# A hybrid decoder layer on one core: the convolution's norm written inside the value projection, and two weight blobs of the output projection read through the projections' staging buffers

## The chip, the cores and the metric

The kernel runs on one core of one Trainium2 chip. The metric is the device time of one execution in microseconds (us). An execution consists of the span that the profile shows, from the first to the last instruction, and about 2 us around it.

The engines that matter here are TensorE (PE in the profile, with PEld for its weight loads), VectorE (DVE), ScalarE (ACT) and SyncE (SP), which issues the weight loads. GpSimd (POOL) issues the transfers of the feed-forward part only. Each engine works through its own list of instructions in order and waits at an instruction whose operands aren't ready.

## The reference

One decoder layer, 512 tokens, width 2048, all in float32:

```python
h = modulate(rms_norm(x, norm1_g), sh1, sc1)
u = h @ w_in
u_b, u_c, u_h, q, kc, vc, ksl, vsl, kwn, vwn, gl = split(u)
y_conv = u_b * causal_depthwise_conv3(u_c * u_h)          # 1024 channels
y_attn = nsa_attention(q, k_cmp, v_cmp, k_slc, v_slc, k_win, v_win, sigmoid(gl))   # 8 heads x 128
mixed = concat([rms_norm(y_conv, gnorm_conv_g), rms_norm(y_attn, gnorm_attn_g)])
x = x + g1 * (mixed @ w_out)
h = modulate(rms_norm(x, norm2_g), sh2, sc2)
x = x + g2 * (square(relu(h @ w_ff1)) @ w_ff2)
return rms_norm(x, normf_g)
```

`sh1, sc1, g1, sh2, sc2, g2` are the six parts of `silu(c) @ w_ada + b_ada`.

## The kernel before

**Precision.** A float32 product is made of three fast matmuls. Each operand is split into a high part (`Copy` into the type fp32r on ScalarE) and a low part (the difference, on VectorE). `mm3` (L93 to L95) issues high x high, one mixed product and the other mixed product. A weight blob of 128 x 1024 (or 1072) numbers is therefore loaded by SyncE, copied by ScalarE (`wh`, L83) and subtracted by VectorE (`wl`, L84) before TensorE can use all of it.

**Staging.** In the first part of the kernel all weights go through one pool, `stage`: three `raw` buffers for the load (L73), two `wh` and two `wl`. A new load waits until a raw buffer has been read, and a new `wh` until TensorE is done with the blob two places before. In the last part (from L740 on) a second pool, `ffp`, has six `rw` buffers for the loads (L755) and three `hl` tiles for the split halves (`hilo`, L763 and L764). `ffp` is opened after the pools of the first part (`att`, `front`) are closed, and lies in the memory that they leave; a buffer of it that lies on an older one waits for the last use of that one.

**Who sets the order.** Up to L362 the program keeps the order in which it is written (`pin`). Behind that a list scheduler orders each engine's instructions; it takes the order of the source as a priority and moves single instructions past each other where it thinks them ready. Buffers are handed out from the free ones.

**The stages around the change.**

- The convolution (L487 to L514) makes eight channel tiles `y`, and adds their squares into `sacc`. The last projection of it ends the convolution's matmuls.
- `row_norm` (L167, called at L518 for the convolution) needs `sacc`: four small matmuls against a column of ones (L170), a square root on ScalarE with its table load (L177), a reciprocal (L178) and a diagonal tile `dg` (L188) on VectorE, one 512-column matmul that spreads the result over the partitions (L191), and a copy of it to `rc` (L181). `rc` is used by `mixed` (L555), eight VectorE instructions.
- The values and gates (L521 to L544): eight blobs of `w_v`, two groups `g` of four blocks `blk`, here called V0 to V7. A blob feeds 48 matmuls of 268 columns. With each blob the loop asks for one column of the modulation (`more_ada`: two loads of `w_ada` and two VectorE dot products, L133). Behind the fourth blob of a group the four banks are split into `vv` (L539, L540) and the gates are made (L543, with a table load for Tanh, and L544).
- The queries (L570 on), then the attention (L592 to L722), with 16 calls of `out_conv` (L602) spread over it; each call loads and splits one blob of `w_oc` and has 24 matmuls of 512 columns, and every second one also loads two tiles of `x` into a raw buffer, which L614 reads.
- Behind the attention its eight heads are normalized (L730) and split into `mixa` (L89, L90), with the last two calls of `out_conv`, 14 and 15, in between (L727 to L737).
- The attention's part of the output projection (L784 to L790): eight blobs of `w_oa`, here A0 to A7, each with 24 matmuls of 512 columns into eight banks. Then eight blobs of `w_oa2`, and the feed-forward part, which takes the larger half of the time.

The two loops that the change touches, before:

```python
    rc = accum("rc")
    row_norm(bank, sacc, 1024, rc)                                  # L518
...
    for k in range(8):
        wh, wl = hilo(hl_tile(), raw_blob(a["w_oa"][k]))            # L787
        for i in range(8):
            s = slice(i * P, (i + 1) * P)
            mm3(pm[i], wh[:, s], wl[:, s], mixa[k][:, 0], mixa[k][:, 1], k == 0, k == 7)
```

Of the kernel before, what the change touches and what calls it, by code (L numbers as in the profile page):

```python
# [40 lines left out]
def hybrid_layer(ctx: ExitStack, tc: tile.TileContext, a, out):  # L41
# [11 lines left out]
    def slot(dtype=F32, name="m"):  # L53
        return mainp.tile([P, SLOT], dtype, name=name, tag="m")

    def pair(dtype=F32, name="m"):
        return slot(dtype, name)[:, :2 * T].rearrange("p (a b) -> p a b", a=2)
# [4 lines left out]
    def accum(name="sacc"):  # L62
        return small.tile([P, T], F32, name=name, tag="acc2k", bufs=2)
# [3 lines left out]
    def pin(ins):  # L67

        return tc.keep_in_program_order(ins) if pinned[0] else ins

    def load(src, cols=1024):
        raw = stage.tile([P, BLOB], F32, name="raw", bufs=3)
        pin(nc.sync.dma_start(out=raw[:, :cols], in_=src))  # L73
        return raw

    def weights(src, cols=1024, spare=False):
        raw = load(src, cols)
        if spare:
            wh, wl = slot(F32R, name="swh"), slot(F32R, name="swl")
        else:  # L80
            wh = stage.tile([P, BLOB], F32R, name="wh")
            wl = stage.tile([P, BLOB], F32R, name="wl")
        pin(nc.scalar.activation(wh[:, :cols], raw[:, :cols], AF.Copy))  # L83
        pin(nc.vector.tensor_tensor(out=wl[:, :cols], in0=raw[:, :cols], in1=wh[:, :cols].bitcast(F32),  # L84
                                    op=OP.subtract))
        return wh, wl

    def split(dst, src):
        pin(nc.scalar.activation(dst[:, 0], src, AF.Copy))  # L89
        pin(nc.vector.tensor_tensor(out=dst[:, 1], in0=src, in1=dst[:, 0].bitcast(F32), op=OP.subtract))  # L90

    def mm3(ps, lh, ll, rh, rl, start, stop, more=False):
        pin(nc.tensor.matmul(ps, lh, rh, start=start, stop=False, skip_group_check=more))  # L93
        pin(nc.tensor.matmul(ps, lh, rl, start=False, stop=False, skip_group_check=more))  # L94
        pin(nc.tensor.matmul(ps, ll, rh, start=False, stop=stop, skip_group_check=more))  # L95
# [71 lines left out]
    def row_norm(bank, square, width, dst, t0=0, t1=NQ):  # L167
        total = bank()
        for t in range(t0, t1):
            nc.tensor.matmul(total[:, t:t + 1], square[:, t * P:(t + 1) * P], ones[:, 0:1],  # L170
                             start=True, stop=True)
        row_bcast(bank, total[:, t0:t1], width, dst[:, t0 * P:t1 * P])

    def row_bcast(bank, total, width, dst):
        n = total.shape[-1]
        rs = small.tile([P, NQ], F32, name="rs")[:, :n]
        pin(nc.scalar.activation(rs, total, AF.Sqrt, scale=1.0 / width, bias=eps))  # L177
        pin(nc.vector.reciprocal(rs, rs))  # L178
        ps = spread(bank, rs)
        if dst is not None:  # L180
            nc.scalar.activation(dst, ps[:, :n * P], AF.Copy)  # L181
        return ps
# [26 lines left out]
    def bank():  # L209
        return psp.tile([P, T], F32, name="ps")  # L210
# [104 lines left out]
    for s, (name, k) in enumerate(steps):  # L315
# [5 lines left out]
        wh, wl = w  # L321
# [41 lines left out]
    def more_ada(n, early=True):  # L363
        for _ in range(min(n, len(todo))):
            ada(todo.pop(0), early)
# [118 lines left out]
    sacc = None  # L484
    for j in range(8):
# [22 lines left out]
        if j == 0:  # L508
            sacc = accum()
# [5 lines left out]
    while background:  # L515
        tick()
    rc = accum("rc")
    row_norm(bank, sacc, 1024, rc)  # L518


    gates = attc.tile([P, NQ, NG, NR, 3], F32, name="gates")  # L521
# [1 line left out]
    for g in range(NG):  # L523
        pv = [bank() for _ in range(NQ)]
        for blk in range(4):
            wh, wl = weights(a["w_v"][g * 4 + blk], BLOB)
            more_ada(1)
            for j in range(4):
                k = blk * 4 + j
                s = slice(j * 268, (j + 1) * 268)  # L530
                for t in range(NQ):
                    c = slice(t * P, (t + 1) * P)
                    mm3(pv[t][:, :268], hs[k][:, 0, c], hs[k][:, 1, c], wh[:, s], wl[:, s],
                        k == 0, k == NK - 1)
        for t in range(NQ):
            if t % 2 == 0:
                vp = pair(F32R, name="vv").rearrange("p h (t c) -> p h t c", t=2)
            vv[g, t] = vp[:, :, t % 2]
            nc.scalar.activation(vv[g, t][:, 0], pv[t][:, :256], AF.Copy)  # L539
            nc.vector.tensor_tensor(out=vv[g, t][:, 1], in0=pv[t][:, :256],  # L540
                                    in1=vv[g, t][:, 0].bitcast(F32), op=OP.subtract)
            gt = gates[:, t, g].rearrange("p r b -> p (r b)")
            nc.scalar.activation(gt, pv[t][:, 256:268], AF.Tanh, scale=0.5)  # L543
            nc.vector.tensor_scalar(gt, gt, 1.0, 0.5, op0=OP.add, op1=OP.mult)  # L544
# [25 lines left out]
    for g in range(NG):  # L570
        pq = [bank() for _ in range(NR)]
        for k in range(NK):
            if k % 2 == 0:
                wh, wl = weights(a["w_q"][g * 8 + k // 2])
# [30 lines left out]
    def out_conv(m):  # L605
        if m % 2 == 0:
            x1.append(pair(name="x1"))
            out_conv.x = load(a["xt"][m // 2].rearrange("p a b -> p (a b)"))
        ps = psw.tile([P, T], F32, name="pw")
        wh, wl = weights(a["w_oc"][m])  # L610
        for k in range(8):
            s = slice(k * P, (k + 1) * P)
            mm3(ps, wh[:, s], wl[:, s], mix[k][:, 0], mix[k][:, 1], k == 0, k == 7)
        nc.vector.scalar_tensor_tensor(out=x1[m // 2][:, m % 2], in0=ps, scalar=col(M_G1, m),  # L614
                                       in1=out_conv.x[:, (m % 2) * T:(m % 2 + 1) * T],
                                       op0=OP.mult, op1=OP.add)
# [111 lines left out]
    for j in range(8):  # L728
        y = ya[j]
        nc.vector.scalar_tensor_tensor(out=y, in0=y, scalar=vec[:, V_GA + j:V_GA + j + 1], in1=ra,  # L730
                                       op0=OP.mult, op1=OP.mult)
        mt = pair(F32R, name="mixa")
        split(mt, y)
        mixa.append(mt)
        if j % 4 == 0:
            out_conv(m)
            m += 1  # L737
    att.close()
    front.close()

# [12 lines left out]
    def raw_blob(src):  # L753
        raw = ffp.tile([P, 1024], F32, name="rw", bufs=6)
        nc.sync.dma_start(out=raw, in_=src)  # L755
        return raw

    def hl_tile():
        t = ffp.tile([P, 2, 1024], F32R, name="hl", bufs=3)
        return t[:, 0], t[:, 1]  # L760

    def hilo(dst, src):
        nc.scalar.activation(dst[0], src, AF.Copy)  # L763
        nc.vector.tensor_tensor(out=dst[1], in0=src, in1=dst[0].bitcast(F32), op=OP.subtract)  # L764
        return dst
# [18 lines left out]
    sacc = accum()  # L784
    pm = [bankf() for _ in range(8)]
    for k in range(8):
        wh, wl = hilo(hl_tile(), raw_blob(a["w_oa"][k]))  # L787
        for i in range(8):
            s = slice(i * P, (i + 1) * P)
            mm3(pm[i], wh[:, s], wl[:, s], mixa[k][:, 0], mixa[k][:, 1], k == 0, k == 7)  # L790
# [212 lines left out]
    sacc = accum()  # L1003
# [193 lines left out]
```

## Time and profile before

| | |
|---|---|
| time, median of 3 runs | 2250.53 us (2250.18 to 2252.56) |
| the profiled execution's own time | 2251.69 us |
| its span | 2249.9 us |
| busy: VectorE, ScalarE | 1919.1 us (85%), 1009.5 us (45%) |
| moved by DMA | 453.62 MB, 202 GB/s in the mean |
| mean granted TensorE clock | 0.974 |

In a row of the timeline the first two numbers are the start and the duration in us, then come the engine, the line of the kernel, the operation, output and input tiles, shapes and the count of merged instructions; in brackets stand the engine's idle time before it and what ended that. Successive matmuls overlap: a row's duration is longer than the step from one matmul to the next. In a row of the table by stretches come the stretch, its length, the busy time (and count) of PE, PEld, DVE, ACT and POOL, the granted TensorE clock as a share of full speed, the DMA engines' share and GB/s.

### The profile page before, as it was taken

The page shows a single profiled execution, that of the slowest core. Times are in us where ns is not written, and L with a number is a line of the kernel's source. Part 1 is how long each engine was busy: PE and PEld are TensorE (multiplying, and loading weights), DVE is VectorE, ACT ScalarE, POOL GpSimd, SP SyncE. Part 2 cuts the span into 40 slices and gives each one's busy share as a digit, 9 for nine tenths or more (in the row PEclk, how much of TensorE's full clock was granted, in tenths as well). Part 3 has the DMA queues.
Part 4 walks back from the last instruction along what each step waited for, and adds up shares of the span by engine and source line. Part 5 has one row for each costly group of instructions (what it writes and reads, how often), then busy time and mean ns, then how long its engine had stood idle before and what let it go on. Part 6 is the DMA issues. An engine that isn't in the chain of part 4 may idle for free.

```text
span 2249.9 us, 37644 instructions
## 1 busy us (share of the span) xinstructions
PE 2138.4 (95%) x14942; PEld 1976.7 (88%) x14942; DVE 1919.1 (85%) x2998; ACT 1009.5 (45%) x1468; POOL 193.5 (9%) x366
## 2 busy tenths in 40 slices
PE   6999699999999999899999999999899999999996
PEld 4777478788877769799999999999899999999996
DVE  8889988776586755999999999999899999999995
ACT  4431233222354433766665666656433333333353
POOL 0000000000000000021111111113211011001100
PEclk8999799999999999899999999999999999999998
DMA  8988378756211134176666666668865466366432
GB/s 345 337 319 312 135 287 349 286 210 247 91 50 57 57 113 167 68 223 200 201 206 202 201 195 197 196 207 256 325 244 186 161 234 235 124 224 243 168 114 94
DMA packets 143984, 453.62 MB, mean 202 GB/s; under 512 B 15808, under 2 KB 20160, under 8 KB 143808
## 3 DMA queue, kind: packets, MB, share of 16 engines
q1 hardware_dynamic: 92192, 323.27, 40.2%
q0 software_dynamic: 51616, 127.95, 17.1%
q8 instruction: 117, 1.92, 0.3%
q14 instruction: 59, 0.48, 0.1%
HBM read 383.00 MB, written 68.16 MB: 201 GB/s over the span
## 4 chain that ended last, share of the span: by engine, by line
PE 78%; DVE 13%; ACT 4%; DMA 3%; issue 2%; SPq 0%; DVEq 0%; ACTq 0%
PE pf L93 19%; PE pf L95 19%; PE pf L94 19%; PE ps L95 5%; PE ps L94 5%; PE ps L93 5%; DVE scr L133 3%; DVE wl L84 2%; DMA wa<-in_w_ada 1%; PE pw L94 1%; PE pw L95 1%; PE pw L93 1%; DVE hl L764 1%; PE pt L683 1%; ACT wh L83 1%
## 5 line engine op out<-in xcount | busy, mean ns | idle before, releaser
L95 PE MATMUL pf<-tk,hl 128*128 128x256 f32 x3576 | 1007.1, 282 | 13.0 <-DVE hl L764 13.0
L93 PE MATMUL pf<-tk,hl 128*128 128x256 f32 x3576 | 1009.7, 283 | 9.6 <-ACT hl L763 8.2
L94 PE MATMUL pf<-tk,hl 128*128 128x256 f32 x3576 | 1007.1, 282 | 1.2 <-DVE tk L834 1.2
L95 PEld LDWEIGHTS pf<-tk,hl 128*128 128x128 f32 x3576 | 677.9, 190 | 15.6 <-DVE hl L764 15.5
L93 PEld LDWEIGHTS pf<-tk,hl 128*128 128x128 f32 x3576 | 679.2, 190 | 12.2 <-ACT hl L763 10.9
L94 PEld LDWEIGHTS pf<-tk,hl 128*128 128x128 f32 x3576 | 678.1, 190 | 1.6 <-DVE tk L834 1.5
L763 ACT ACTIVATE hl<-rw 128x1024 fp32r<-128x1024 f32 x266 | 280.8, 1057 | 291.6 <-PE pf L95 266.8
L764 DVE TENSOR_TENSOR hl<-rw,hl 128x1024 fp32r<-128x1024 f32 x266 | 324.5, 1221 | 48.4 <-ACT hl L763 48.0
L763 ACT ACTIVATE hl<-sg 128x1024 fp32r<-128x1024 f32 x189 | 200.4, 1061 | 268.6 <-PE pf L95 241.7
L764 DVE TENSOR_TENSOR hl<-sg,hl 128x1024 fp32r<-128x1024 f32 x189 | 230.8, 1222 | 42.2 <-ACT hl L763 42.1
L133 DVE SCALAR_TENSOR_TENSOR scr<-wa,cs 128x1024 bf16<-128x1024 f32 x192 | 229.7, 1220 | 6.2 <-DMA wa<-in_w_ada 6.1
L83 ACT ACTIVATE wh<-raw 128x1024 fp32r<-128x1024 f32 (+1 forms) x103 | 108.8, 1060 | 238.9 <-PE ps L94 137.9
L84 DVE TENSOR_TENSOR wl<-raw,wh 128x1024 fp32r<-128x1024 f32 (+1 forms) x103 | 126.2, 1227 | 54.9 <-ACT wh L83 54.1
L837 DVE TENSOR_TENSOR sg<-sg,rw 128x1024 f32<-128x1024 f32 x126 | 153.6, 1219 | 0.9
L95 PE MATMUL ps<-h_m,wl 128*128 128x512 f32 x360 | 143.0, 397 | 4.9 <-DVE wl L84 4.8
L93 PE MATMUL ps<-h_m,wh 128*128 128x512 f32 x360 | 142.6, 396 | 1.5 <-DVE part L346 1.0
L94 PE MATMUL ps<-h_m,wh 128*128 128x512 f32 x360 | 141.7, 394 | 0.0
L1011 DVE SCALAR_TENSOR_TENSOR x<-pf,mod,x 128x256 f32<-128x256 f32 x256 | 120.2, 480 | 15.6 <-PE pf L95 12.6
L95 PE MATMUL ps<-h,wl 128*128 128x512 f32 x280 | 114.4, 409 | 17.4 <-DVE wl L84 17.3
L93 PE MATMUL ps<-h,wh 128*128 128x512 f32 x280 | 113.3, 405 | 6.0 <-ACT wh L83 3.2
L94 PE MATMUL ps<-h,wh 128*128 128x512 f32 x280 | 113.1, 404 | 0.0
L977 POOL DMA_DIRECT2D g<-gt x192 | 100.9, 532 | 86.6 <-DVE gt L834 81.6
(306 smaller groups left out, 2971.9 us busy)
## 6 DMA issues: line engine op xcount, KB each, us to landing
rw<-in_w_f SPq DMA_DIRECT2D x262, 512.0 KB, 4.3
wa<-in_w_ada SPq DMA_DIRECT2D x192, 512.0 KB, 6.4
tk<-g POOLq DMA_DIRECT2D x114, 512.0 KB, 8.4
g<-gt POOLq DMA_DIRECT2D x192, 256.0 KB, 5.1
raw<-in_w_conv SPq DMA_DIRECT2D x32, 512.0 KB, 7.2
g<-gb POOLq DMA_DIRECT2D x36, 256.0 KB, 2.3
raw<-in_w_kv SPq DMA_DIRECT2D x16, 512.0 KB, 5.3
raw<-in_w_cv SPq DMA_DIRECT2D x16, 512.0 KB, 5.6
```

The lines of the kernel that those rows point to most:

```text
L83: pin(nc.scalar.activation(wh[:, :cols], raw[:, :cols], AF.Copy))
L84: pin(nc.vector.tensor_tensor(out=wl[:, :cols], in0=raw[:, :cols], in1=wh[:, :cols].bitcast(F32), op=OP.subtract))
L93: pin(nc.tensor.matmul(ps, lh, rh, start=start, stop=False, skip_group_check=more))
L94: pin(nc.tensor.matmul(ps, lh, rl, start=False, stop=False, skip_group_check=more))
L95: pin(nc.tensor.matmul(ps, ll, rh, start=False, stop=stop, skip_group_check=more))
L133: pin(nc.vector.scalar_tensor_tensor(out=scr, in0=w, scalar=1.0, in1=cs[i].rearrange("p a b -> p (a b)"), op0=OP.mult, op1=OP.mult, accum_ ...
L683: nc.tensor.transpose(pt[:, r * P:(r + 1) * P], probs[b, r][:, kb * P:(kb + 1) * P], ident)
L763: nc.scalar.activation(dst[0], src, AF.Copy)
L764: nc.vector.tensor_tensor(out=dst[1], in0=src, in1=dst[0].bitcast(F32), op=OP.subtract)
L837: nc.vector.tensor_tensor(out=dst, in0=x, in1=y, op=op)
L977: nc.gpsimd.dma_start(out=gd[p // 4][idx[j]][p % 4 // 2][:, p % 2], in_=g[:, j])
L1011: nc.vector.scalar_tensor_tensor(out=xm, in0=src, scalar=gate, in1=xm, op0=OP.mult, op1=OP.add)
```

## The change

The call of `row_norm` for the convolution moves from ahead of the value projection into its loop, behind the matmuls of V1. The first two blobs of `w_oa` are loaded and split with `weights`, that is through the buffers of `stage`, before the pools of the first part are closed; the loop over `w_oa` takes them from there and the other six as before. No arithmetic is added or left out.

```diff
@@ -515,7 +515,6 @@
     while background:
         tick()
     rc = accum("rc")
-    row_norm(bank, sacc, 1024, rc)
 
 
     gates = attc.tile([P, NQ, NG, NR, 3], F32, name="gates")
@@ -532,6 +531,8 @@
                     c = slice(t * P, (t + 1) * P)
                     mm3(pv[t][:, :268], hs[k][:, 0, c], hs[k][:, 1, c], wh[:, s], wl[:, s],
                         k == 0, k == NK - 1)
+            if g == 0 and blk == 1:
+                row_norm(bank, sacc, 1024, rc)
         for t in range(NQ):
             if t % 2 == 0:
                 vp = pair(F32R, name="vv").rearrange("p h (t c) -> p h t c", t=2)
@@ -735,6 +736,7 @@
         if j % 4 == 0:
             out_conv(m)
             m += 1
+    oa = [weights(a["w_oa"][k]) for k in range(2)]
     att.close()
     front.close()
 
@@ -784,7 +786,7 @@
     sacc = accum()
     pm = [bankf() for _ in range(8)]
     for k in range(8):
-        wh, wl = hilo(hl_tile(), raw_blob(a["w_oa"][k]))
+        wh, wl = oa[k] if k < 2 else hilo(hl_tile(), raw_blob(a["w_oa"][k]))
         for i in range(8):
             s = slice(i * P, (i + 1) * P)
             mm3(pm[i], wh[:, s], wl[:, s], mixa[k][:, 0], mixa[k][:, 1], k == 0, k == 7)
```

## The prediction

> **What bounds the kernel now.** I read the page, the chain that ended last, TensorE's timeline at both edited places, the stretches with their granted clock, and VectorE's, ScalarE's and SyncE's timelines there.
>
> ```profile
> span 2249.9 us, 37644 instructions
> PE 2138.4 (95%) x14942; PEld 1976.7 (88%) x14942; DVE 1919.1 (85%) x2998; ACT 1009.5 (45%) x1468; POOL 193.5 (9%) x366
> PE 78%; DVE 13%; ACT 4%; DMA 3%; issue 2%; SPq 0%; DVEq 0%; ACTq 0%
> ```
>
> TensorE is busy for 95% of the span and holds 78% of the chain. An edit pays where TensorE stands still or is slowed. The first place is the convolution's end:
>
> ```profile
> 461.00 0.39 PE L94 MATMUL ps<-h_m,wh 128*128 128x512 f32 x1
> 461.23 0.40 PE L95 MATMUL ps<-h_m,wl 128*128 128x512 f32 x1
> 464.49 1.26 PE L170 MATMUL ps<-ones,sacc 128*128 128x1 f32 x8 [2.87 <-DVE sacc L514]
> 467.04 2.07 PE L191 MATMUL ps<-dg,ones 128*128 128x512 f32 x2 [1.29 <-DVE dg L188]
> 468.12 1.21 PE L93 MATMUL ps<-wh,h 128*128 128x268 f32 x1
> 472.16 0.28 PE L93 MATMUL ps<-wh,h 128*128 128x268 f32 x1
> 499.86 0.29 PE L93 MATMUL ps<-wh,h 128*128 128x268 f32 x1
> 468.00:472.00 4.00, 4.00 (x16) 3.43 (x15) 4.00 (x10) 0.60 (x1) 0.00 (x0) 0.50 0.00 0
> 472.00:476.00 4.00, 4.00 (x35) 4.00 (x34) 3.26 (x7) 0.00 (x0) 0.00 (x0) 1.00 0.00 0
> ```
>
> The norm's matmuls stand ahead of V0 in TensorE's list, so V0 waits through their two waits (2.87 and 1.29 us). V0 then runs at half the granted clock until about 472: its first 15 matmuls take 472.16 - 468.12 = 4.04 us. The full-clock step is (499.86 - 472.16) / 225 = 0.123 us, 225 matmuls lying between V0's 16th and V5's first. 512-column matmuls step by 461.23 - 461.00 = 0.23.
>
> The second place is the start of A0:
>
> ```profile
> 817.20 0.40 PE L95 MATMUL pw<-mix,wl 128*128 128x512 f32 x1
> 822.66 0.80 PE L93 MATMUL pf<-mixa,hl 128*128 128x512 f32 x1 [5.07 <-ACT hl L763]
> 823.92 0.80 PE L95 MATMUL pf<-mixa,hl 128*128 128x512 f32 x1
> 830.48 0.40 PE L93 MATMUL pf<-mixa,hl 128*128 128x512 f32 x1
> 822.60:826.70 4.10, 4.00 (x9) 2.73 (x10) 3.50 (x3) 1.91 (x3) 0.00 (x0) 0.50 1.02 403
> ```
>
> TensorE idles 5.07 us for A0's high copy, again runs at half clock afterwards, and reaches A1 at 830.48.
>
> **The norm, part by part.** In the order of the built program V0 follows the convolution directly, the four L170 stand behind V1's 96th value matmul, and L191 behind 29 more. Nothing else is added; each engine's count is unchanged. Times below are on the old clock.
>
> ```profile
> 808.85 1.10 PE L191 MATMUL pt<-dg,ones 128*128 128x512 f32 x2
> 920.25 0.61 PE L170 MATMUL pf<-ones,sacc 128*128 128x1 f32 x4 [1.35 <-DVE sacc L773]
> 462.56 1.27 DVE L84 TENSOR_TENSOR wl<-raw,wh 128x1072 fp32r<-128x1072 f32 x1 [0.20 <-ACT wh L83]
> 466.90 1.22 DVE L133 SCALAR_TENSOR_TENSOR scr<-wa,cs 128x1024 bf16<-128x1024 f32 x1
> 468.04 1.22 DVE L133 SCALAR_TENSOR_TENSOR scr<-wa,cs 128x1024 bf16<-128x1024 f32 x1
> 476.47 1.10 ACT L83 ACTIVATE wh<-raw 128x1072 fp32r<-128x1072 f32 x1 [6.73 <-PE ps L95]
> 480.86 3.40 DVE L555 SCALAR_TENSOR_TENSOR y<-y,vec,rc 128x512 f32<-128x512 f32 x5
> 493.47 1.16 DVE L540 TENSOR_TENSOR vv<-ps,vv 128x256 fp32r<-128x256 f32 x3 [2.81 <-ACT vv L539]
> 494.19 1.28 ACT L543 ACT_TABLE_LOAD   x1
> ```
>
> Gain: V0 can start at 461.5, so its 16th matmul at 461.5 + 15 x 0.123 = 463.3 instead of 472.16: 8.8 us. About 2.2 of it (4.04 - 1.85) is the half clock.
>
> Paid back: at full clock four L170 records took 0.61, eight cost 1.0 to 1.2; L191 1.1. I take 2.1 together, which leaves 6.7.
>
> Do the splits keep up? V1's low half had been subtracted by 463.8 before; two dot products (468.04 - 466.90 = 1.14 each) and the last sum of squares, 0.6, now precede it: 466.7 at most, and V1 begins at 461.5 + 5.9 = 467.4. V3's copy and the square root's table load now stand ahead of the root on ScalarE: V1 ends at 473.3, copy 1.10, load 1.28, then the old 1.29 from sums to `dg`: 477.2. TensorE reaches L191 at 473.3 + 1.0 + 29 x 0.123 = 477.9. No wait, 0.7 us to spare.
>
> The new wait is at V5. V2 ends at 461.5 + 144 x 0.123 + 2.1 = 481.3. Behind that, in series: V4's copy to 482.6 and subtraction to 483.9; five `mixed` steps, now late because `rc` is, at 0.67 to 487.3; four `vv` subtractions to 488.8; a `mixed` step, 489.5; four gates, which wait for V3's end at 487.2, four copies and the Tanh load (1.28), to 489.9; two `mixed` steps, 491.2; two dots, 493.5; V5's subtraction, 494.7. TensorE gets to V5 at 493.1 and has four high matmuls there before it needs the low half, 493.6. The wait is 1.1 us; bounds 0 and 2.2 (the same chain with its idle moments squeezed out, or as many again). V6 to V7 have their halves over 2 us early. Part one: 6.7 - 1.1 = **5.6 us**, between 4.5 and 6.7.
>
> The Trainium skill ("TensorE: Matmul & The Clock Gate", "Part 1: The HAM clock gate", "What's actually happening") lets the clock fall to half after an idle window of about 3.4 us. Here gaps of 2.87 and 1.29 us with work between them were followed by 0.50, so the trace doesn't keep to it. By the rule alone the 2.2 us would have nothing to do with these gaps, part one would be 3.4 and the time 2241.2.
>
> **The two blobs.**
>
> ```profile
> 805.33 0.75 DVE L614 SCALAR_TENSOR_TENSOR x<-pw,mod,raw 128x512 f32<-128x512 f32 x1 [0.23 <-PE pw L95]
> 811.41 1.96 ACT L89 ACTIVATE mixa<-ya 128x512 fp32r<-128x512 f32 x3 [0.82 <-DVE ya L730]
> 813.88 1.28 DVE L90 TENSOR_TENSOR mixa<-ya,mixa 128x512 fp32r<-128x512 f32 x2
> 819.53 1.41 DVE L730 SCALAR_TENSOR_TENSOR ya<-ya,vec,rc 128x512 f32<-128x512 f32 x2
> 821.03 1.35 DVE L90 TENSOR_TENSOR mixa<-ya,mixa 128x512 fp32r<-128x512 f32 x2
> 821.57 2.94 ACT L763 ACTIVATE hl<-rw 128x1024 fp32r<-128x1024 f32 x3
> 822.64 3.50 DVE L764 TENSOR_TENSOR hl<-rw,hl 128x1024 fp32r<-128x1024 f32 x3 [0.25 <-ACT hl L763]
> L755 SPq DMA_DIRECT2D rw<-in_w_oa x1: 328/328/328, 817.6 to 817.6; - x1
> DMA to landing us min/median/max: 3.4/3.4/3.4
> ```
>
> A0's load waits for the raw buffer that L614 of `out_conv(13)` reads, so it starts at 806.1 and lands 3.4 later. Its high copy stands behind the first head's copy, 812.1 to 813.1, and moves the next two heads by about 1 us, which VectorE doesn't feel (it took them at 813.9 and later). A1's copy waits for `out_conv(15)`'s matmuls (817.6), and the copies of heads 6 and 7 queue behind it; they are wanted some 30 us later.
>
> The built order gives TensorE 14 high matmuls of A0 (seven banks, L93 and L94) right behind 817.20: 817.4 to 820.7. The first L95 needs A0's low half, which VectorE has placed behind the last two L730: 820.9 + 1.2 = 822.1. Ten matmuls remain: 822.1 + 2.3 = 824.4 for A1's start against 830.48. Gain 6.0 us. The idle shrinks to 1.4 us, and I take the clock to stay up; then some 2 us of the gain is the half-clock stretch.
>
> What is late next: A2's load. Its buffer lies on A0's staging memory and now waits for A0's last high matmuls, 824.4. It lands at 827.8; copy 1.0, subtraction 1.2: 830.1. A1 ends at 824.4 + 5.6 = 830.0 and A2's first L95 comes at 830.5. A3's load waits for A1's last matmul, leads a burst of five exactly like the row at 817.6, and gives its low half at 836.0; wanted at 836.1. I charge 0.1 for both. Upper bound from the next row below: a first landing of 4.8 instead of 3.4 makes each 1.4 later, 2.4 together after the spare time. From A4 on the waits for buffers are the old ones. Part two: **5.9 us**, between 3.6 and 6.0.
>
> **Sum.** 5.6 + 5.9 = 11.5. The rest is carried by a busy TensorE, with compute-released waits that shift along. The profiled execution took 2251.69 (span 2249.9 and 1.8 around it): 2240.2. The median of the runs is 1.16 lower, so I forecast **2239.0 us**.
>
> **The rivals.**
>
> ```profile
> 325.27 0.50 PE L95 MATMUL ps<-h,wl 128*128 128x512 f32 x1 [1.57 <-DVE wl L84]
> 327.00:329.00 2.00, 2.00 (x10) 1.65 (x9) 2.00 (x5) 1.71 (x2) 0.00 (x0) 1.00 0.40 160
> 703.28 0.38 PE L703 MATMUL pt<-ones,sr 128*128 128x1 f32 x2 [1.12 <-DVE sr L701]
> 704.00:711.00 7.00, 6.99 (x26) 5.85 (x26) 4.67 (x24) 2.55 (x10) 0.00 (x0) 0.51 0.00 0
> DMA to landing us min/median/max: 4.8/8.2/11.2
> ```
>
> A, the clock falls in the new waits. A lone gap of 1.57 us at 325 left the clock at 1.00, but 1.12 us at 703 among smaller ones brought 7 us at 0.51. One drop of about 3.4 us (half of that 7) costs 1.7; both waits 3.4: 2242.4.
>
> B, V5 waits for its dots' loads. The last row is the burst of eight `w_ada` loads at 491, which now starts at 484, and the first two of it feed the dots ahead of V5. In order they should land first, at 4.8; if they land last, at 11.2, V5 waits 4.2 more: 2243.2.
>
> C, the change doesn't do what it says at A0: if the raw buffer comes free only with `out_conv(15)`'s L614, at 819, the load lands at 822.4 and TensorE starts about 1 us later than before: 2251.69 - 5.6 + 1.0 - 1.16 = 2245.9. The built order names the earlier buffer, which speaks against it.
>
> D, slower. Before, A1 to A5 were requested at once; now A2 and A3 are each requested only when TensorE is one blob away. Both gain parts are eaten when each load takes (11.5 / 2) + 3.4 = 9.2 us or more; at the 11.2 of a full burst they cost 7.7 each: 2239.0 + 15.4 = 2254.4. No other transfers run then, which speaks against it.
>
> **How the numbers follow.** Forecast 0.72, A 0.10, B 0.08, C 0.06, D 0.04. The best bounds give 12.7, 2237.8; the worst 8.1, 2242.4; the three runs before spread over 2.4 us, half on each side. With A and B the range is 2236 to 2244.5. About 0.2% (4.5 us) is what a measurement tells from no change: faster, below 2246.0, takes the forecast, A, B and half of C, 0.93, less 0.03 for a wait that I haven't seen: 0.90; same 0.05; slower, D and 0.01 of the unseen, 0.05.
>
> **What would show it.** In the profile after: no idle before L170 or L191, and no half-clock stretch near 470; V5's first L94 waiting about 1 us for VectorE's L84; A0's first L95 waiting about 1.5 us with clock 1.00 behind it; A2 and A3 without idle above 0.5; both new loads landing in about 3.4. I am wrong if TensorE waits over 2 us at V5, A2 or A3, or if the time between the two places, or from A4 to the end, isn't the old one within 2 us.

## The result and the profile after

The changed kernel took 2241.84 us in the median of five runs (2240.88 to 2245.57), the kernel before 2252.13 us in the five runs beside it. The ratio is 0.9959, with a 95% interval from 0.9944 to 0.9973. The prediction was 2239.0 us, in a range from 2236 to 2244.5. Against the median it was made from, that is a ratio of 0.9949, which lies inside the interval. In microseconds the medians differ by 10.3 where 11.5 were forecast. Two later sets of runs of the same kernel gave ratios of 0.9945 and 0.9952.

The page of the changed kernel begins with the span and the engines' busy times; the third line is the sum of the chain that ended last.

```profile
span 2242.1 us, 37644 instructions
PE 2136.3 (95%) x14942; PEld 1975.0 (88%) x14942; DVE 1917.8 (86%) x2998; ACT 1009.5 (45%) x1468; POOL 193.6 (9%) x366
PE 78%; DVE 13%; ACT 4%; DMA 3%; issue 2%; POOL 0%; SPq 0%; DVEq 0%; ACTq 0%; POOLq 0%
```

Nothing changes in these sums: the same number of instructions, the same bound. The 7.8 us that the span lost are found only at the places. The first place, in TensorE's timeline of the changed kernel:

```profile
462.77 0.39 PE L95 MATMUL ps<-h_m,wl 128*128 128x512 f32 x1
463.00 0.29 PE L93 MATMUL ps<-wh,h 128*128 128x268 f32 x1
474.85 0.95 PE L170 MATMUL ps<-ones,sacc 128*128 128x1 f32 x8
479.33 1.02 PE L191 MATMUL ps<-dg,ones 128*128 128x512 f32 x2
495.76 0.39 PE L94 MATMUL ps<-wl,h 128*128 128x268 f32 x1 [0.78 <-DVE wl L84]
```

V0 starts one matmul step behind the convolution, L170 and L191 have no bracket (no wait), and V5's first L94, the fifth matmul of V5, waits 0.78 us. From the last convolution matmul to this place it is 495.76 - 462.77 = 32.99 us. In the kernel before, V5's fifth matmul was

```profile
500.35 0.28 PE L94 MATMUL ps<-wl,h 128*128 128x268 f32 x1
```

which makes 500.35 - 461.23 = 39.12 us. The stretches of the same kernel (clock third from the right) show full clock for V0 and the first part of V1; from 471 to 483 it is 1.00 as well:

```profile
463.00:467.00 4.00, 4.00 (x34) 3.99 (x33) 3.79 (x7) 1.59 (x2) 0.00 (x0) 1.00 0.73 285
467.00:471.00 4.00, 4.00 (x35) 4.00 (x34) 4.00 (x7) 1.10 (x1) 0.00 (x0) 1.00 0.42 141
```

The second place, again from the timeline of the changed kernel, and one row of VectorE among TensorE's:

```profile
813.42 0.40 PE L95 MATMUL pw<-mix,wl 128*128 128x512 f32 x1
813.66 0.39 PE L93 MATMUL pf<-mixa,wh 128*128 128x512 f32 x1
817.10 1.22 DVE L84 TENSOR_TENSOR wl<-raw,wh 128x1024 fp32r<-128x1024 f32 x1
818.37 1.90 PE L95 MATMUL pf<-mixa,wl 128*128 128x512 f32 x7 [1.36 <-DVE wl L84]
820.80 0.39 PE L93 MATMUL pf<-mixa,wh 128*128 128x512 f32 x1
```

A0 starts at once, its first L95 waits 1.36 us for VectorE's subtraction, and A1 starts 820.80 - 813.42 = 7.38 us behind the last `out_conv` matmul, against 13.28 before.

The prediction had no row for a third place, the first matmul of the attention's first `out_conv`. Before, it followed the last matmul of the queries (606.43) without a gap:

```profile
606.66 0.40 PE L93 MATMUL pw<-mix,wh 128*128 128x512 f32 x1
```

In the changed kernel's timeline:

```profile
602.17 1.05 ACT L83 ACTIVATE wh<-raw 128x1024 fp32r<-128x1024 f32 x1
603.12 0.59 ACT L585 ACTIVATE qr<-ps 128x512 f32<-128x512 f32 x1
603.76 0.51 PE L93 MATMUL pw<-mix,wh 128*128 128x512 f32 x1 [1.42 <-ACT qr L585]
```

TensorE waits 1.42 us for the copy of the last query head, which stands behind a weight copy on ScalarE.

So the span's -7.8 us is made up as follows: +1.54 ahead of the change (the convolution ends at 462.77 instead of 461.23), -6.13 at the first place, +0.81 from V5 to the last `out_conv` matmul (+1.69 up to the first `out_conv` matmul, where the new wait is, and -0.88 behind it), -5.90 at the second place, and +1.9 from A1 to the end, of which 0.25 is the wait of A3 for its late load. The first and the rest of the last are in code that the change doesn't touch; what is known of them stands at the end.

### The profile page after: what moved, and what is told of

The parts are those of the page before. It is cut to its first block, busy times and chain, and to the rows that moved or that the text cites. A ratio compares the mean times of both kernels' runs of the same rounds, so it can differ in the third digit from the quotient of the medians.

```text
span 2242.1 us, 37644 instructions
## 1 busy us (share of the span) xinstructions
PE 2136.3 (95%) x14942; PEld 1975.0 (88%) x14942; DVE 1917.8 (86%) x2998; ACT 1009.5 (45%) x1468; POOL 193.6 (9%) x366
## 4 chain that ended last, share of the span: by engine, by line
PE 78%; DVE 13%; ACT 4%; DMA 3%; issue 2%; POOL 0%; SPq 0%; DVEq 0%; ACTq 0%; POOLq 0%
PE pf L95 19%; PE pf L93 19%; PE pf L94 19%; PE ps L95 5%; PE ps L94 5%; PE ps L93 5%; DVE scr L133 3%; DVE wl L84 2%; DMA tk<-g 1%; PE pw L93 1%; PE pw L95 1%; PE pw L94 1%; ACT wh L83 1%; PE pt L684 1%; DVE hl L766 1%
## 5 line engine op out<-in xcount | busy, mean ns | idle before, releaser
L95 PE MATMUL pf<-tk,hl 128*128 128x256 f32 x3576 | 1006.9, 282 | 12.4 <-DVE hl L766 12.4
L94 PE MATMUL pf<-tk,hl 128*128 128x256 f32 x3576 | 1007.3, 282 | 1.4 <-DVE tk L836 1.4
L95 PEld LDWEIGHTS pf<-tk,hl 128*128 128x128 f32 x3576 | 677.9, 190 | 14.8 <-DVE hl L766 14.8
L94 PEld LDWEIGHTS pf<-tk,hl 128*128 128x128 f32 x3576 | 678.3, 190 | 1.8 <-DVE tk L836 1.6
L95 PE MATMUL ps<-h_m,wl 128*128 128x512 f32 x360 | 143.1, 397 | 4.7 <-DVE wl L84 4.6
L94 PE MATMUL ps<-h_m,wh 128*128 128x512 f32 x360 | 141.7, 394 | 0.0
L95 PE MATMUL ps<-h,wl 128*128 128x512 f32 x280 | 115.1, 411 | 17.2 <-DVE wl L84 17.1
L94 PE MATMUL ps<-h,wh 128*128 128x512 f32 x280 | 113.4, 405 | 0.0
```

## The experiments

Twelve runs were made. Two stretches are read from each trace: C-O, from the last convolution matmul to the first `out_conv` matmul, and the waits at A0 and A1. Ratios are to the kernel before on the same chip. "Pools" in a name means that the bank exchange of the run pools is in it too; the two kernels called best have it as well.

| kernel | ratio, 95% interval | C-O, us | waits at A0, A1, us |
|---|---|---|---|
| before | 1 | 145.43 | 5.07, none |
| the change | 0.9959 [0.9944, 0.9973] | 140.99 | 1.36, none |
| norm_only | 0.9983 [0.9974, 0.9992] | 141.01 | 5.08, none |
| stage_only | 0.9972 [0.9962, 0.9982] | 145.45 | 1.35, none |
| after_again | 0.9945 [0.9932, 0.9957] | 141.01 | 1.36, none |
| pools | 0.9937 [0.9923, 0.9950] | 139.43 | 1.32, none |
| norm_split | 0.9973 [0.9963, 0.9982] | 145.85 | 1.35, none |
| v0_pools | 0.9944 [0.9931, 0.9957] | 138.39 | 1.33, none |
| j4_pools | 0.9934 [0.9922, 0.9946] | 139.42 | none, none |
| oa1_pools | 0.9978 [0.9969, 0.9987] | 139.42 | 1.34, 4.65 |
| v3_pools | 0.9964 [0.9951, 0.9978] | 142.35 | 1.33, none |
| best_v0_j4 | 0.9938 [0.9925, 0.9950] | 138.39 | none, none |
| best_v2_j4 | 0.9930 [0.9917, 0.9943] | 138.42 | none, none |
| after_third | 0.9952 [0.9939, 0.9966] | 141.01 | 1.37, none |

In the three profiles of the changed kernel these stretches repeat within 0.02 us; the ratios have intervals of about ±0.0013, which is ±3 us. The verdicts below rest on the stretches.

**The norm's move alone.** The staging is taken out again:

```diff
-    oa = [weights(a["w_oa"][k]) for k in range(2)]
...
-        wh, wl = oa[k] if k < 2 else hilo(hl_tile(), raw_blob(a["w_oa"][k]))
+        wh, wl = hilo(hl_tile(), raw_blob(a["w_oa"][k]))
```

> The norm's move alone; w_oa as before. Theory: between the last convolution matmul and V5's first L94 TensorE saves 6.1 us as it did in the changed kernel (39.12 to 32.99), V5 waits 0.8 us, and the new wait at the first out_conv matmul (1.42 us on the copy of the last query head, L585) belongs to the norm's move, since moving the norm's two PSUM tiles shifts the banks: 6.1 - 1.4 = 4.7 us faster than before, ratio 0.998. At A0 the old 5.07 us of idle and the half clock stay. Rival 1: that wait comes from the staging or from the run: 6.1 us faster, no wait at the attention's start. Rival 2: only the gaps and not the half clock are saved by the move: 3.4 - 1.4 = 2.0 us faster, and a half-clock stretch stays somewhere in V0 to V3.

In its timeline:

```profile
459.50 0.39 PE L95 MATMUL ps<-h_m,wl 128*128 128x512 f32 x1
492.49 0.40 PE L94 MATMUL ps<-wl,h 128*128 128x268 f32 x1 [0.77 <-DVE wl L84]
600.51 0.51 PE L93 MATMUL pw<-mix,wh 128*128 128x512 f32 x1 [1.42 <-ACT qr L585]
815.66 0.80 PE L93 MATMUL pf<-mixa,hl 128*128 128x512 f32 x1 [5.08 <-ACT hl L764]
```

It is 492.49 - 459.50 = 32.99 us to V5's first L94, the same as in the changed kernel, and the wait at the attention's start is there. C-O is 4.4 us shorter than before, where the theory said 4.7; the ratio allows 2 to 6 us. So the move itself brings the wait, and rival 1 is out. Rival 2 would have left the half clock in: the granted clock is 1.00 in every stretch from 459.5 to 495.

**The staging alone.** The norm's call goes back ahead of the value projection:

```diff
     rc = accum("rc")
+    row_norm(bank, sacc, 1024, rc)
...
-            if g == 0 and blk == 1:
-                row_norm(bank, sacc, 1024, rc)
```

> Staging of A0 and A1 alone; the norm ahead of V0 as before. Theory: the waits of 2.87 and 1.29 us and the half clock at V0 are back, the attention starts without a wait, A0's first L95 waits 1.4 us at full clock, and 5.9 us are saved between the last out_conv matmul and A1 (13.28 to 7.38): ratio 0.9974. Rival: part of the saving at A0 needs the norm's move (another order of ScalarE's copies ahead): under 4 us. Rival: the two parts are not additive and this one gives 7 us or more.

```profile
466.05 1.51 PE L170 MATMUL ps<-ones,sacc 128*128 128x1 f32 x8 [2.86 <-DVE sacc L514]
468.85 2.08 PE L191 MATMUL ps<-dg,ones 128*128 128x512 f32 x2 [1.29 <-DVE dg L188]
823.39 1.90 PE L95 MATMUL pf<-mixa,wl 128*128 128x512 f32 x7 [1.35 <-DVE wl L84]
```

In this timeline the two old waits are back, A0 behaves as in the changed kernel, and the attention starts without a wait (C-O 145.45, as before). The parts are independent: alone they save 4.42 (C-O, norm_only) and 5.92 us (the last `out_conv` matmul to A1, stage_only), in the changed kernel 4.44 and 5.90.

**The changed kernel again, and the banks.** The first of these is unchanged. The second exchanges the two lines that open the pools:

```diff
-    psw = att.enter_context(tc.tile_pool(name="psw", bufs=2, space=PSUM, reuse_waits="tile"))
     pss = att.enter_context(tc.tile_pool(name="pss", bufs=3, space=PSUM, reuse_waits="tile"))
+    psw = att.enter_context(tc.tile_pool(name="psw", bufs=2, space=PSUM, reuse_waits="tile"))
```

> The changed kernel on the same chip as the others. Theory: norm_only and stage_only add up: 4.7 + 5.9 = 10.6 us faster than before (ratio 0.9953), within 1 us. Rival: the parts share something (the half clock at one place depends on the gaps at the other): more than 2 us off the sum.

> The changed kernel with the two lines that open the PSUM pools psw and pss exchanged; the order of instructions on every engine is the same, only the banks differ: the first out_conv now takes bank 3 instead of bank 0, which the last query head fills. Theory: the 1.42 us wait at the first out_conv matmul is a matter of this bank and goes; 1.4 us faster than the changed kernel, 12.0 us faster than before (ratio 0.9947). Rival: that matmul waits for the weights' low half anyway (L84 ends about when the copy does): the same as the changed kernel within 0.4 us, with the wait under another name.

The timeline of pools at the same place, ScalarE's rows and TensorE's first `out_conv` matmul:

```profile
600.64 1.05 ACT L83 ACTIVATE wh<-raw 128x1024 fp32r<-128x1024 f32 x1
601.59 0.59 ACT L585 ACTIVATE qr<-ps 128x512 f32<-128x512 f32 x1
600.64 0.40 PE L93 MATMUL pw<-mix,wh 128*128 128x512 f32 x1
```

ScalarE does the same in the same order, but TensorE starts 0.95 us ahead of the last head's copy instead of behind it, since the first `out_conv` no longer writes into that head's bank. C-O falls by 141.01 - 139.43 = 1.58 us. The cause is settled, though the profile doesn't print bank numbers: the wait comes with the norm's move and goes with the exchange of banks. The norm takes two PSUM tiles (the banks into which the matmuls of this kernel write), and taking them later hands the last query head the bank that the first `out_conv` gets. In norm_split, below, only the second of the two is taken later, and the 1.42 us are there too. The sum of the two parts from their ratios, 0.9983 and 0.9972, is 0.9955; the changed kernel beside them had 0.9945, the same within the intervals.

**Which gap made the half clock.** On top of stage_only the norm is taken apart:

```diff
-    row_norm(bank, sacc, 1024, rc)
+    total = bank()
+    for t in range(NQ):
+        nc.tensor.matmul(total[:, t:t + 1], sacc[:, t * P:(t + 1) * P], ones[:, 0:1], start=True, stop=True)
...
+            if g == 0 and blk == 0:
+                row_bcast(bank, total[:, :NQ], 1024, rc)
```

> Staging as in the changed kernel; the norm taken apart: its four L170 matmuls ahead of V0 as before, the rest behind V0's 48 matmuls. So the 2.87 us gap stands alone and the 1.29 us gap ahead of L191 is gone. It tells what made the half clock at V0. Theory (the gap of 2.87 with only the tiny L170 matmuls behind it isn't enough; it takes both gaps): V0 to V1 at full clock, the last convolution matmul to V5 takes 39.12 - 1.29 - 2.2 = 35.6 us. Rival 1 (the first gap alone drops the clock): 39.12 - 1.29 = 37.8 us and a half-clock stretch of about 4 us. The Trainium skill's rule (TensorE: Matmul & The Clock Gate, Part 1, an idle window of about 3.4 us) would have the clock stay up behind this gap, as the theory does, though it has no reason for the drop behind both. The first out_conv matmul again waits 1.4 us, since the two PSUM tiles still move.

Timeline and, below it, stretches of norm_split:

```profile
458.87 0.40 PE L95 MATMUL ps<-h_m,wl 128*128 128x512 f32 x1
461.79 1.56 PE L520 MATMUL ps<-ones,sacc 128*128 128x1 f32 x8 [2.53 <-DVE sacc L514]
463.21 0.57 PE L93 MATMUL ps<-wh,h 128*128 128x268 f32 x1
```

```profile
460.50:462.50 2.00, 0.71 (x5) 0.71 (x5) 2.00 (x4) 1.46 (x2) 0.00 (x0) 0.91 0.57 234
462.50:464.50 2.00, 2.00 (x10) 2.00 (x11) 1.97 (x6) 0.27 (x1) 0.00 (x0) 0.50 0.03 10
...
468.50:470.50 2.00, 2.00 (x16) 2.00 (x16) 1.22 (x3) 0.00 (x0) 0.00 (x0) 0.88 0.00 0
```

The theory fell, rival 1 holds: to V5's fifth matmul it takes 37.95 us, against 37.8 by rival 1 and 35.6 by the theory. Of the first stretch 0.91 is 1.64 us at full and 0.36 at half clock, so the clock fell at 462.1; by the last row it came back at 469.0. The first gap, 2.53 us here, with 1.4 us of tiny matmuls behind it was enough, and V0 ran at half clock for longer than before, because it started earlier within the low time. The trace of the kernel before says the same:

```profile
464.00:466.00 2.00, 1.26 (x8) 1.17 (x8) 0.43 (x1) 0.56 (x2) 0.00 (x0) 0.80 0.67 226
```

By this 0.80 the clock fell at 465.2, while the second gap began only at 464.49 + 1.26 = 465.75. Without the wait at the attention's start (1.4), C-O is 144.4, only 1.0 below the kernel before. To keep V0 at full clock the norm's first step had to leave the front as well.

**The norm behind V0.**

```diff
-            if g == 0 and blk == 1:
+            if g == 0 and blk == 0:
```

> As pools, but the norm is called behind V0 instead of behind V1: rc is there 5.9 us earlier, five of the mixed steps stand ahead of V4's subtraction, and L191 stands 29 matmuls behind L170 as before. Theory (V5 waits because the mixed steps come late): no wait over 0.2 us at V5, none at V4; ScalarE's V2 copy, table load and root end about when TensorE gets to L191, a wait of 0.3 there at most; the last convolution matmul to V5 takes 32.99 - 0.78 = 32.2, the whole 0.5 to 0.8 us faster than pools. Rival: VectorE simply has too much to do in V0 to V4, and the wait shows at V4 or at L191 instead: 33.0 or more.

VectorE's and TensorE's rows in the timeline of v0_pools:

```profile
468.67 0.95 PE L170 MATMUL ps<-ones,sacc 128*128 128x1 f32 x8
473.13 1.02 PE L191 MATMUL ps<-dg,ones 128*128 128x512 f32 x2
485.28 2.74 DVE L556 SCALAR_TENSOR_TENSOR y<-y,vec,rc 128x512 f32<-128x512 f32 x4
491.30 1.28 DVE L84 TENSOR_TENSOR wl<-raw,wh 128x1072 fp32r<-128x1072 f32 x1 [0.55 <-ACT wh L83]
```

Neither L170 nor L191 waits, V4 and V5 don't either, and VectorE even waits 0.55 us for V5's copy. C-O is 138.39, 1.04 less than pools; 0.78 of it is the wait itself. The order of VectorE's list was the cause of V5's wait, not the amount of its work. Between V4's subtraction and V5's there stand eight `mixed` steps and two dot products in the changed kernel, and four `mixed` steps and no dot product here; this run doesn't tell the two apart.

**A0's low half earlier.**

```diff
         if j % 4 == 0:
             out_conv(m)
             m += 1
-    oa = [weights(a["w_oa"][k]) for k in range(2)]
+        if j == 4:
+            oa = [weights(a["w_oa"][k]) for k in range(2)]
```

> As pools, but the two weights calls for A0 and A1 stand in the loop over the eight heads, behind out_conv(15) in the source and ahead of heads 5 to 7. In the built order A0's high and mixed matmuls are no longer pulled apart, and A0's low half is subtracted earlier. Theory: the 1.36 us wait at A0's first L95 goes, the last out_conv matmul to A1 takes 24 x 0.233 = 5.6 plus little, about 6.0 instead of 7.38: 1.4 us faster than pools. Rival: VectorE is the bound there, and the delayed heads make A1 or A2 wait for mixa instead: no gain over pools within 0.3.

In the timeline of j4_pools:

```profile
810.85 0.40 PE L95 MATMUL pw<-mix,wl 128*128 128x512 f32 x1
813.08 1.22 DVE L84 TENSOR_TENSOR wl<-raw,wh 128x1024 fp32r<-128x1024 f32 x1
816.66 0.40 PE L93 MATMUL pf<-mixa,wh 128*128 128x512 f32 x1
```

VectorE's row here is already A1's subtraction. A1 starts 816.66 - 810.85 = 5.81 us behind the last `out_conv` matmul, against 7.38: no wait at A0, and none for a head at A1 or A2. VectorE had room, only its order was wrong. In the timed ratio (0.9934 against 0.9937 for pools) the 1.57 us don't show.

**One blob instead of two.** The list of `oa` and the condition in the loop go from 2 to 1:

```diff
-    oa = [weights(a["w_oa"][k]) for k in range(2)]
+    oa = [weights(a["w_oa"][k]) for k in range(1)]
...
-        wh, wl = oa[k] if k < 2 else hilo(hl_tile(), raw_blob(a["w_oa"][k]))
+        wh, wl = oa[k] if k < 1 else hilo(hl_tile(), raw_blob(a["w_oa"][k]))
```

> As pools, but only A0 goes through the staging buffers and A1 through the later pool as before. Theory: nearly the whole gain of the second part is A0's early load; A1's load starts when the memory comes free at out_conv(15)'s end, lands in 3.4 and is split about 5.7 us after the last out_conv matmul, when TensorE is 7.4 behind it: no wait over 0.5 at A1, and no request for A2 that comes late: the same as pools within 0.5 us. Rival: both staged blobs are needed, A1's first matmuls wait 1 us or more for their halves.

SyncE, ScalarE and TensorE in the timeline of oa1_pools:

```profile
818.01 0.40 PE L95 MATMUL pf<-mixa,wl 128*128 128x512 f32 x1
818.25 7.73 SPq L757 DMA_DIRECT2D rw<-in_w_oa  x8
821.95 1.06 ACT L765 ACTIVATE hl<-rw 128x1024 fp32r<-128x1024 f32 x1 [6.62 <-DMA rw<-in_w_oa]
823.06 0.80 PE L93 MATMUL pf<-mixa,hl 128*128 128x512 f32 x1 [4.65 <-ACT hl L765]
```

A clear miss. A1's load is issued at 818.25, when A0's last matmul has begun, not at `out_conv(15)`'s end 7.4 us earlier, which fits a buffer on memory that A0's staging still holds. It lands 3.7 us later (818.25 to 821.95), the copy takes 1.06, and TensorE waits 4.65 us; the row's 0.80 for a matmul shows the half clock again. The staged blobs hold up the loads behind them, so one more staged blob must run meanwhile: a blob takes 5.6 us on TensorE, and load, copy and subtraction take 3.7 + 1.06 + 1.2 = 6.0. With two blobs this covers all but some tenths.

**Later, without matmuls in between.**

```diff
-            if g == 0 and blk == 1:
+            if g == 0 and blk == 3:
```

> As pools, but the norm is called behind V3. In the built order L191 then follows L170 with no value matmul in between, since the group ends there. It tells whether the gain of the first part comes from being later or from the 29 matmuls between the two steps of the norm. Theory: it's the matmuls in between. L170 waits for nothing, L191 for a root that now queues behind the copies of vv and a table load on ScalarE: a gap of 1.3 (the old one) + 1.3 (table load) + about 1 of copies, 3 to 4 us, which drops the clock more often than not for one or two windows of 3.4 us (by norm_split and before); rc is late and V5 no longer waits. The last convolution matmul to the first out_conv matmul takes 139.43 - 0.78 + 3.5 = 142.2 at full clock, up to 145.5 with the half clock; some 3 to 6 us slower than pools. Rival: being out of the way of V0 is all that matters: the same as pools within 1 us.

Timeline and stretches of v3_pools:

```profile
487.32 0.95 PE L170 MATMUL ps<-ones,sacc 128*128 128x1 f32 x8
490.47 1.92 PE L191 MATMUL ps<-dg,ones 128*128 128x512 f32 x2 [2.20 <-DVE dg L188]
```

```profile
490.50:492.50 2.00, 2.00 (x4) 0.97 (x5) 1.67 (x6) 1.67 (x6) 0.00 (x0) 0.54 1.03 416
492.50:494.50 2.00, 2.00 (x12) 2.00 (x12) 2.00 (x4) 0.52 (x1) 0.00 (x0) 0.60 1.03 422
```

C-O is 142.35 (142.2 expected), 2.9 us more than pools, but not quite for the reason given: the gap is 2.20 us instead of 3 to 4, and the clock fell for about 3.4 us (from 0.16 into the first stretch to 0.40 ahead of the end of the second). The place alone gains little: it is the matmuls between L170 and L191 that hide the norm.

**All three together.** Two kernels: j4 and the exchanged pools with the norm behind V0 or behind V2, and the changed kernel beside them.

> All three together: norm behind V0, psw and pss exchanged, A0 and A1 split inside the loop over the heads. Theory: the savings add. From the last convolution matmul to the first out_conv matmul 138.4 us (v0_pools), from the last out_conv matmul to A1 5.8 us (j4_pools): 1.0 + 1.3 = 2.3 us faster than pools, about 2235.5 us, ratio to before 0.993. Rival: with one of the waits gone the next one up takes over (V4's subtraction behind four mixed steps, or A4 waiting for its load): under 1 us faster than pools.

> As best_v0_j4, but the norm behind V2: rc comes 5.9 us later than in the changed kernel, and only four of the eight mixed steps stand ahead of V5's subtraction in the built order. Theory: the same chain ahead of V5 is some 2.7 us shorter, so no wait at V5 either; 138.4 us to the first out_conv matmul, the same as best_v0_j4 within 0.3. Rival: the chain ahead of V5 hangs on rc, not on the number of steps behind it; with rc later V5 waits longer than 0.8 us, 140 us or more.

> The changed kernel beside the other three on the same chip. Theory: best_v0_j4 is faster by the bank's 1.5, V5's 1.0 and A0's 1.3 us, together 3.8 us.

Both have C-O at 138.4, and A1 starts 5.78 us behind the last `out_conv` matmul. By the stretches they save 141.01 - 138.4 = 2.6 and 7.37 - 5.78 = 1.6, 4.2 us in all. Their medians are 2237.98 and 2237.86 us against 2240.57 for the changed kernel: 2.6 and 2.7 us less, with intervals that overlap its own. The 2235.5 us expected of best_v0_j4 were not reached: its ratio, 0.9938, is that of pools (0.9937). In the profiles the code from the first to the last `out_conv` matmul took 210.35 us in best_v0_j4 and 208.64 in pools, and 208.83 to 210.17 in three executions of the changed kernel; this scatter is of the size of the gains. The norm behind V2 does as well as behind V0: there, too, only four `mixed` steps stand between V4's subtraction and V5's, with three dot products among them, so what counts is that not all eight steps stand there, not when `rc` comes. By the stretches these are the best versions found, but no timing here tells them from pools or j4_pools, and the timed gain over the changed kernel isn't outside the scatter.

## Why the prediction was right, and what it missed

**Part one, 5.6 us predicted, 6.13 measured.** V0 followed the convolution, the clock stayed at 1.00, and L170 and L191 cost 0.95 and 1.02 (2.1 taken together, 1.97 measured) without a wait. V5's wait was named with its cause; it was 0.78 us instead of 1.1, within the bounds of 0 and 2.2. The norm behind V0 and behind V2 bears out the chain of `mixed` steps as its cause. Rival B did not happen: the two dot products ahead of V5's subtraction ran without a wait for their loads. One sum of the prediction is slightly off without consequence: 473.3 + 1.10 + 1.28 + 1.29 is 477.0, not 477.2.

**The clock.** That 2.2 us of part one were the half clock, and that it goes with the gaps, was right; had it nothing to do with them, part one would have given 3.4. The prediction put it down to both gaps with the work between them, and the theory of norm_split said that it took both; that is wrong: norm_split shows that the first alone does it. Rival A, the clock falling in the new waits, did not happen: 0.78 and 1.36 us, and the 1.42 us that nobody had foreseen, left it at 1.00 in the stretches of four us around them, in the changed kernel and in its two repetitions.

**Part two, 5.9 us predicted, 5.7 measured.** Up to A1's start the gain was 5.90, where 6.0 was forecast. The 1.4 us wait at A0's first L95 was 1.36. A2 had no wait. A3's load cost 0.25 on the way from A3 to A4 (5.85 us instead of 5.60 for the step), 0.1 was charged. So up to A4 the gain was 5.68. Rivals C and D are refused: the first load went out at 802.34, at the end of `out_conv(13)`'s residual, and landed in 3.5 us; the second took 4.6 instead of 3.4 and was still early; the late loads landed in time but for these 0.25 us. The missed expectation for one blob shows how near D was: the same rule that was applied to A2 in the prediction holds for A1 there, and costs 4.65 us.

**The step that failed** is "The rest is carried by a busy TensorE, with compute-released waits that shift along." Between the two places a new wait of 1.42 us came up at the first `out_conv`. The prediction followed the instruction orders, buffers and queues, but not the PSUM banks that tiles get when two of them are taken later. Of the 11.5 us forecast the places gave 6.13 + 5.68 = 11.8; C-O, with the wait in it, fell by only 4.44, so that the stretches give 4.44 + 5.68 = 10.1, 1.4 less than forecast. That the medians' 10.3 comes so near to this is partly luck, since a ratio is sure to about 3 us. The rest of the difference to the first timing, 2241.84, is no larger than the scatter; the second set gave 2240.21 and the third 2240.57.

## What to carry to other kernels

When a norm or another short chain interrupts the matmuls, it isn't enough to move it: put independent matmuls between its steps, as many as the chain takes, and look at what the helper engines then have ahead of the next operand. When a tile is taken earlier or later, follow which physical bank or buffer every later tile receives, up to the next stage: an unchanged instruction order can hide a new wait. Memory that is used for an early load is taken from the loads behind it; count whether the blob in hand lasts until the next is loaded and split.

## What the runs showed of the hardware

**The half clock lasted 3.4 or 6.8 us, and not always the same in the same kernel.** In norm_split it lasted from 462.1 to 469.0. In two executions of the very same changed kernel, the same gap early in the attention had different effects. Stretches of the changed kernel, as first profiled:

```profile
620.00:622.00 2.00, 0.27 (x1) 0.30 (x2) 1.96 (x4) 0.00 (x0) 0.00 (x0) 0.82 0.00 0
622.00:624.00 2.00, 2.00 (x9) 1.91 (x9) 1.99 (x5) 0.63 (x1) 0.00 (x0) 0.50 0.00 0
...
628.00:630.00 2.00, 2.00 (x17) 1.87 (x16) 1.42 (x9) 0.87 (x4) 0.00 (x0) 0.97 0.54 207
```

And of after_again:

```profile
620.00:622.00 2.00, 1.74 (x10) 1.52 (x11) 2.00 (x5) 0.63 (x1) 0.00 (x0) 0.93 0.00 0
...
624.00:626.00 2.00, 2.00 (x10) 1.65 (x10) 2.00 (x6) 1.64 (x7) 0.00 (x0) 0.71 0.00 0
```

The first fell at 621.3 and came back at 628.1, 6.8 us; the second fell at 621.7 and came back at 625.2, 3.4 us. In both the gap was about 2.45 us. The Trainium skill ("TensorE: Matmul & The Clock Gate", "Part 1: The HAM clock gate", "What's actually happening") says that activity is counted in windows of about 3.4 us that run freely and don't start with the work. One and two such windows fit the 3.4 and 6.8 measured here. That gaps of 2.2 to 2.9 us amid tiny matmuls lowered the clock would then be a question of what a window as a whole contains; this was not tested, and how much work keeps the clock up was not measured.

**The scatter ahead of the change.** The code up to the end of the convolution is the same in all kernels, yet its last matmul started between 458.87 (norm_split, shown above) and 463.41 (v3_pools):

```profile
463.41 0.39 PE L95 MATMUL ps<-h_m,wl 128*128 128x512 f32 x1
```

From 260 to 280 us TensorE was busy for 19.03 us at a granted clock of 0.90 in norm_split, and for 15.56 us at 0.78 in v3_pools:

```profile
260.00:280.00 20.00, 19.03 (x95) 15.48 (x96) 17.41 (x27) 6.79 (x8) 0.00 (x0) 0.90 0.67 241
```

```profile
260.00:280.00 20.00, 15.56 (x70) 12.31 (x71) 15.78 (x24) 8.15 (x9) 0.00 (x0) 0.78 0.63 215
```

So part of the spread arises here, with more idle time and a lower clock together; which of them made how much was not separated. The +1.5 us ahead of the change in the first comparison lies within this spread of 4.5 us, and so in size does the +1.9 behind A1; where the latter comes from, beyond the 0.25 at A3, was not shown.
